# Sample-token convolution taps as GpSimd products with VectorE sums, and another order of projections in the first mixer

## The chip, the cores and the metric

The kernel runs on one core of a Trainium2 chip. The metric is the time of one execution on the device in microseconds (us), the median of 3 runs. The core's engines are called as the profile calls them: PE (TensorE; PEld is its weight load), DVE (VectorE), ACT (ScalarE), POOL (GpSimd), and SP (SyncE), which issues most transfers. Each takes its own instructions in one fixed order.

## What is computed

One inference step of a two-layer decoder trunk for 512 prompt tokens and 8 sequences of 4 sample tokens, 544 columns in all; the layout is channels on partitions, tokens along the free axis. Only the first layer's mixer is touched by the change. Cut to that:

```python
def causal_depthwise(ext, w, b):                 # 31 taps, one filter a channel
    y = lax.conv_general_dilated(ext, w[:, None, :].astype(ext.dtype), (1,), 'VALID',
                                 dimension_numbers=('NWC', 'WIO', 'NWC'),
                                 feature_group_count=ext.shape[-1])
    return y + b.astype(ext.dtype)

def mixer_ab(x, conv_st, shift_st, wkv_st, w_in, conv_w, conv_b, ln_g, ln_b, ...):
    p = x @ w_in
    pa, pb = p[..., :2 * D_A], p[..., 2 * D_A:]
    u = pa[..., :D_A] * jax.nn.sigmoid(pa[..., D_A:])
    ext = jnp.concatenate([conv_st.astype(u.dtype), u], axis=1)
    ya = jax.nn.silu(layer_norm(causal_depthwise(ext, conv_w, conv_b), ln_g, ln_b)).astype(f32)
    ...
    r, k, v, wl, al, gl = jnp.split(q, SPLIT_B, axis=-1)     # q: pb after the token shift
    ...
    y, new_wkv = wkv_recurrence(r, k, v, decay, kk, a, wkv_st)
    ...
    out = jnp.concatenate([ya, yb], axis=-1) @ w_out
```

The convolution has 512 channels (four tiles of 128), the recurrence 8 heads of 64 channels (four pairs of heads, one pair a tile).

## The kernel before, in words

The input projection has 22 tiles of 128 output channels: gates and values of the four convolutions (4 to 7 and 0 to 3), r, k and v of the four pairs (8 to 19), and two low-rank tiles (20, 21). A projection is a loop over 8 blocks of 128 input channels in two halves of the columns (256 and 288); each block takes three products (`xh` by `whi`, `xl` by `whi`, `xh` by `wlo`), since weights and inputs are split into a high and a low part. So one projection is 48 products on PE (line 192). The weights come as one stream in the order of `ab_order` (line 305). ACT makes each `whi`, and DVE the `wlo` that belongs to it.

The mixer is written as generators that are emitted in turns by `weave` (line 172): each step of a part has the priority of its turn plus the part's delay (`hi` -4, `md` -6, `lo` 8), and a scheduler then fixes the order of every engine's queue. The parts are these:

- `pair_in(p)`: projections of k, r and v of pair p; DVE and POOL make the operands `ar` and `kb` (line 439 on).
- `pair_front(p)`: PE's products of `ar` and `kb` (line 725) go through DVE to `xa` and `xk`. `xa` goes to DRAM as `dx` and comes back as `xb` by SP's queue, one 16x16 block a partition. POOL inverts the blocks there (`wkv_solve`, line 759) in 30 small steps (`stmp`, `mm`). The result goes back as `dm`, and to its place as `mn`.
- `pair_mid(p)`: PE's products with `mn`; the first of them (line 801) give DVE's `z`.
- `pair_out(p)`: the scan over eight chunks (line 882), group norm and gate, to `yb`.
- `conv_in(i)`: the projections of gate and value; DVE writes `uext` (prompt) and `usam` (30 rows of state and 4 new tokens of 8 sequences).
- `conv_taps(i)`: ACT's first tap and 30 DVE taps into `cacc`, for the prompt's 512 columns and for the samples' 32 columns each (line 167).
- `conv_end`: layer norm over the four convolutions, silu, and the half of the output projection that needs only them (8 tiles of 24 products). The second half needs every pair's `yb`.
- `sample_front`, `sample_out`: the recurrence of the sample tokens, with a solve of its own on POOL.

What holds the mixer's order are the fixed queues: PE meets products with `mn` between those of the projections, POOL has solves and operands in one queue, and DVE has taps, weight splits and evictions in one queue.

Of the kernel before, what the change touches and what calls it, by code (L numbers as in the profile page):

```python
# [15 lines left out]
P = 128  # L16
# [108 lines left out]
class Kernel:  # L125
# [46 lines left out]
    def weave(self, *gens):  # L172
        """emits the steps of (delay, part) in turns; the scheduler takes the step of least turn plus delay first"""
        gens = list(gens)
        while gens:
            for g in list(gens):
                try:
                    with self.tc.high_priority(offset=self.tc.cur_priority - int(200 * (self.turn + g[0]))):
                        next(g[1])
                except StopIteration:  # L180
                    gens.remove(g)
            self.turn += 1

    def order(self, ins):
        """the first product of a bank clears it, the others add to it, the last one ends it"""
        for a, b in [(ins[0], b) for b in ins[1:-1]] + [(a, ins[-1]) for a in ins[1:-1]]:
            self.tc.add_manual_dep(b.ins, a.ins.name, mybir.DependencyInfo(
                mybir.DependencyClass.NoSync, mybir.DependencyReason.DATA), reason="order")

    def mm(self, *a, **k):  # L190
        """a product; while `last` is not None, the tensor engine takes them as they are emitted"""
        ins = self.nc.tensor.matmul(*a, **k)  # L192
        if self.last is not None:
            self.chain(self.last + [ins])
            self.last = [ins]
        elif self.gates:
            # products of the layer norm go between those of the stream as soon as they can
            self.since += 1
            while self.gates and self.since > self.gates[0][0] + GWIDTH:
                self.gates.pop(0)  # L200
            for n, g in self.gates:
                if self.since > n:
                    self.chain([g, ins])
        return ins

    def dma(self, q, out, in_):
        """a transfer; while `lastq` is not None, the queue takes them as they are emitted"""
# [16 lines left out]
    def stream(self, key, ms, parts):  # L224
        """chunks of the m tiles `ms`, taken in turns"""
# [5 lines left out]
    def slot(self, which, i, name):  # L231
        """a tile for chunk i from the pool whose next tile frees first; None while that one is in use"""
# [35 lines left out]
    def gemm_steps(self, tiles, x, halves=(0, 1), look=2, turns=False, keep=False, parts=None, tags=("mm", "mm")):  # L268
        """products of the m tiles `tiles` [(key, m)], k in turns; x(k) -> (hi halves, lo halves)"""
# [27 lines left out]
    def setup(self):  # L297
# [6 lines left out]
        # tiles of w_in_ab: conv value 0-3, gate 4-7, r 8-11, k 12-15, v 16-19, wl|al 20, gl 21  # L304
        self.ab_order = [20, 21, 12, 8, 16, 4, 0, 13, 9, 17, 5, 1, 14, 10, 18, 6, 2, 15, 11, 19, 7, 3]
# [21 lines left out]
    # ================= layer 0: conv | wkv =================  # L327
    def mixer_ab(self):
# [52 lines left out]
        def shifted(m, ps, q):  # L381
            """token shift of tile m (of the RWKV part): q <- (1-mu) p + mu prev"""
# [22 lines left out]
        # until x comes back for the residual, its place holds what lives briefly  # L405
# [22 lines left out]
        def conv_taps(i):  # L428
# [5 lines left out]
            self.act(cs, usam[:, 0:32], AF.Identity, scale=w(0), bias=cb)  # L434
            for t in range(1, 31):
# [3 lines left out]
                self.stt(cs, usam[:, 8 * t:8 * t + 32], w(t), cs, ALU.mult, ALU.add)  # L439
            yield  # L440

        def pair_in(p):
# [17 lines left out]
            # inclusive sums of the log decay within chunks  # L460
# [22 lines left out]
            # keys and keys times rate of a chunk: those of even chunks the other way round  # L483
# [7 lines left out]
            # minus the normalized key, and the key times the in-context rate  # L491
# [19 lines left out]
            # sum over a head of r k r_k, times v  # L511
# [33 lines left out]
        def head_norm(y, parts, bv, gate, out, tag="wi"):  # L545
            """group norm of each head, plus bonus, times gate"""
# [42 lines left out]
        def conv_end():  # L589
            """layer norm over the 512 channels, swish, and what it adds to the residual"""  # L590
# [42 lines left out]
        weave((md, pair_front(0)), (0, conv_in(0)), (0, pair_in(1)))  # L633
        weave((hi, pair_mid(0)), (md, pair_front(1)), (0, conv_in(1)), (0, after(5, pair_in(2))), (lo, conv_taps(0)))
        weave((hi, pair_out(0)), (hi, pair_mid(1)), (md, pair_front(2)), (0, conv_in(2)), (0, after(4, pair_in(3))), (lo, conv_taps(1)))
        weave((hi, pair_out(1)), (hi, pair_mid(2)), (md, pair_front(3)), (0, conv_in(3)), (lo, conv_taps(2)))
        nc.scalar.dma_start(out=O["shift"], in_=shout)
        weave((hi, pair_out(2)), (hi, pair_mid(3)), (md, sample_front()), (lo, conv_taps(3)))
# [27 lines left out]
    def head_rsqrt(self, x, out, scale, v, tag, floor=True):  # L666
        """1 / sqrt(max(s, v)) or 1 / sqrt(s + v), s = scale times the sum over a head of x, on the head's channels"""
# [33 lines left out]
    # channels: (head, channel) on partitions. tokens: those of chunk c = 2 cp + c2 that go with alpha, b and w on  # L701
    # HS[c2], those that go with k and v on the other half
    def blocks(self):
        """chunk, its half, cp, where w and v keep it, head, rows of alpha, b and w, rows of k and v"""
# [4 lines left out]
    def wkv_front(self, d, dx):  # L709
        nc, gp = self.nc, self.gp  # L710
        ar, kb, v = d["ar"], d["kb"], d["v"]
        # per head and chunk: products with alpha and with r, then b and k themselves
# [20 lines left out]
        # tokens on partitions  # L733
# [25 lines left out]
    def wkv_solve(self, dx, dm, nu, mn):  # L759
        """inverses of the unit lower triangular 16-blocks and their transposes, one block a partition"""  # L760
# [30 lines left out]
    def wkv_mid(self, d):  # L791
        """from the inverses of the 16-blocks to (I - X)^-1, then its products with alpha and B"""
# [13 lines left out]
        # the inverses of the 32-blocks: of the first one as it is, of both transposed  # L806
# [13 lines left out]
        # the block between them  # L820
# [26 lines left out]
    def wkv_tail(self, d):  # L847
        nc, gp = self.nc, self.gp
        xk, R, wv, ar, pend = d["xk"], d["R"], d["wv"], d["ar"], d["pend"]
        # of chunk c = 2 cp + c2: [P, c2, cp, 64]  # L850
# [44 lines left out]
    # tokens of pair p on HS[p % 2]: 32 that go with alpha, b and w, then 32 that go with k and v  # L895
# [71 lines left out]
    def sample_end(self, g, ys):  # L967
# [7 lines left out]
        # r and alpha against the states  # L975
# [33 lines left out]
        # new states; what comes from tokens of other sequences is masked out  # L1009
# [18 lines left out]
    # ================= residual and layer norm =================  # L1028
# [10 lines left out]
    def norm_tile(self, m, ps, halves=(0, 1), scaled=False):  # L1039
        """z = ALPHA x + f (scaled: x comes with the factor), kept in xf less the mean of its first tile"""  # L1040
# [33 lines left out]
    def norm_end(self, name, layer, h, out=None):  # L1074
# [7 lines left out]
        with self.tc.high_priority(offset=UP):  # L1082
# [18 lines left out]
            # (y y v - 3) y is -2 times the next y  # L1101
# [48 lines left out]
    # ================= feed-forward =================  # L1150
# [11 lines left out]
    def ffn(self, L, out=None):  # L1162
        nc, tc, I, O = self.nc, self.tc, self.I, self.O
        with tc.tile_pool(name=f"ff{L}", bufs=1) as fp:
# [11 lines left out]
            def value(i, h, hp):  # L1176
                """silu of the causal convolution of half h"""
# [61 lines left out]
    # ================= layer 1: S5 =================  # L1239
    def s5_setup(self, new):  # L1240
        """the discretization; rows 0-63 and 64-127 both hold the 64 states; in the place of tiles written later"""
# [30 lines left out]
        # powers 0..8 of the transition  # L1272
# [13 lines left out]
        # f = (A - 1) / lambda  # L1286
# [14 lines left out]
        # q_j = A^(7-j) f, j = 0..7; p1 = (pr; -pr), p2 = (-pi; -pi), q1 = (qr; qr), q2 = (-qi; qi)  # L1301
# [14 lines left out]
        # eight steps turn by this much, in turns; against it on the rows of imaginary parts  # L1316
# [4 lines left out]
        # sample: A^4 h0  # L1321
# [13 lines left out]
    def s5_systems(self):  # L1335
        """the matrices of all tiles, in the place of the activations, which nothing reads meanwhile"""
# [19 lines left out]
        for m in range(8):  # L1356
# [17 lines left out]
            # impulse responses, 4 groups side by side  # L1374
# [23 lines left out]
    def mixer_c(self, ctx, yp):  # L1398
# [13 lines left out]
        # inputs: states on rows  # L1412
# [9 lines left out]
        def rotations(m):  # L1422
            """by 1..64 times eight steps"""
# [12 lines left out]
        def load_fm(m, q):  # L1436
            """matrices of the 8 groups of tile m: what comes in"""
# [3 lines left out]
        def load_gx(m, q):  # L1441
            """from the states to what goes out"""
# [3 lines left out]
        def load_tm(m, q):  # L1446
            """from what comes in to what goes out"""
# [5 lines left out]
        def value(m, h, ps):  # L1453
            """half h of u: steps of eight on rows"""
# [18 lines left out]
        def states(m):  # L1473
            """what comes in, rotated"""
# [15 lines left out]
        def swapped(e):  # L1490
            """real and imaginary parts exchanged"""
# [159 lines left out]
    def _exp(self, out, x):  # L1651
        """e^x to float32's accuracy: 2^k e^r"""
# [19 lines left out]
    def _sincos(self, sp, x, sn, cs, turns):  # L1672
        """sine and cosine of x, and x in turns less whole ones"""
        V = self.nc.vector
        k, r, z, s, c = (sp() for _ in range(5))
        # quarter turns
# [19 lines left out]
        # quarter q = k mod 4: angle = r + q pi/2, in turns k/4 + r/(2 pi)  # L1696
        V.tensor_scalar(turns, k, 0.25, None, op0=ALU.mult)
        self._frac(turns)  # in -1/2..1/2: -1/2 (or 1/2), -1/4, 0, 1/4
        a, b = self._new(), self._new()
        # cos(q pi/2) = 1 - 4 |t|  and sin(q pi/2) from t  # L1700
        self.stt(a, turns, -1.0, turns, ALU.mult, ALU.max)
        V.tensor_scalar(a, a, -4.0, 1.0, op0=ALU.mult, op1=ALU.add)
        # sin: 4 t where |t| = 1/4, else 0: 4 t (1 - |cos|)
# [155 lines left out]
```

## Time and profile before

| | |
|---|---|
| median of 3 runs | 1547.79 us (1545.06 to 1548.09) |
| the profiled execution's own time (its span) | 1542.7 us |
| its mean granted TensorE clock | 0.953 of 2.4 GHz |
| busy: PE, PEld, DVE, ACT, POOL | 94 %, 89 %, 66 %, 40 %, 23 % of the span |
| first mixer (up to the second half of the output projection) | 0 to 380.93 us |

The span is counted from the first to the last instruction of one profiled execution, while the median belongs to runs without a profile; the two differ by 5.1 us. Busy shares are averages over stages: the mixer that the change touches is a quarter of the span, and its shares are read from stretches of 50 us. An instruction's wait is named by what released it.

### The profile page before, as it was taken

How to read it: one execution, taken by the hardware profiler on the slowest of the kernel's cores; microseconds unless marked ns; L12 is line 12 of the kernel's file. 1: busy time of each engine (PE TensorE's matmuls, PEld its weight loads, DVE VectorE, ACT ScalarE, POOL GpSimd, SP SyncE). 2: the span in 40 equal slices, each digit the busy share in tenths (PEclk: the TensorE clock that was granted, in tenths of full speed). 3: DMA queues.
4: the chain of work that ended last, by engine and by line, in shares of the span. 5: the costliest groups of instructions: out<-in, count | busy, mean ns of one | idle time of the engine just before them, and what ended most of it. 6: DMA issues, size and time to landing. Idle time of an engine off the chain costs nothing.

```text
span 1542.7 us, 31307 instructions
## 1 busy us (share of the span) xinstructions
PE 1445.0 (94%) x12064; PEld 1374.1 (89%) x12064; DVE 1013.4 (66%) x2513; ACT 616.9 (40%) x1407; POOL 353.9 (23%) x492
## 2 busy tenths in 40 slices
PE   7999999789799999999999789999899999999996
PEld 6988887577789999999899778899899999999996
DVE  6688796766879955557884856754675555554335
ACT  5444352251264444443232435553454444442222
POOL 1252552611540200002561622102420000000102
PEclk9999999689899999999999789999999999999997
DMA  5222113111213232225563367832222222232321
GB/s 192 73 65 67 39 54 100 22 38 58 99 37 118 89 127 89 84 85 164 165 182 116 111 178 210 219 107 96 67 69 89 90 89 85 88 92 86 84 68 58
DMA packets 128340, 152.43 MB, mean 99 GB/s; under 512 B 46512, under 2 KB 71856, under 8 KB 127936
## 3 DMA queue, kind: packets, MB, share of 16 engines
q1 hardware_dynamic: 105232, 120.11, 25.7%
q10 hardware_dynamic: 20800, 22.46, 4.6%
q0 software_dynamic: 2160, 7.87, 1.6%
q8 instruction: 95, 1.56, 0.4%
q14 instruction: 53, 0.43, 0.1%
HBM read 128.17 MB, written 22.22 MB: 97 GB/s over the span
## 4 chain that ended last, share of the span: by engine, by line
PE 71%; DVE 11%; DMA 6%; POOL 4%; issue 3%; ACT 3%; SPq 1%; ACTq 0%; DVEq 0%; POOLq 0%
PE ps_mm L192 61%; PE ps_wk L192 3%; POOL stmp L170 2%; DVE xres L170 2%; POOL mm L170 2%; DVE wlo L170 2%; DVE xres L167 1%; DMA tm<-dk 1%; DVE s5a L170 1%; PE ps_wf L725 1%; ACT xres L164 1%; DVE ln_t L167 1%; PE ps_wk L1089 1%; DMA dg<-s5a 1%; DMA ye<-dy 1%
## 5 line engine op out<-in xcount | busy, mean ns | idle before, releaser
L192 PE MATMUL ps_mm<-xh,whi 128*128 128x256 f32 (+1 forms) x2016 | 492.1, 298 | 21.9 <-ACT whi L262 6.5
L192 PE MATMUL ps_mm<-xl,whi 128*128 128x256 f32 (+1 forms) x2016 | 493.2, 296 | 5.2 <-DVE xl L167 3.6
L192 PE MATMUL ps_mm<-xh,wlo 128*128 128x256 f32 (+1 forms) x2016 | 490.0, 295 | 0.0
L170 DVE TENSOR_TENSOR wlo<-wraw,whi 128x512 fp32r<-128x512 f32 x350 | 258.4, 740 | 272.3 <-ACT whi L262 270.1
L262 ACT CAST whi<-wraw 128x512 fp32r<-128x512 f32 x380 | 230.9, 611 | 514.7 <-PE ps_mm L192 448.9
L192 PEld LDWEIGHTS ps_mm<-xh,whi 128*128 128x128 f32 x2016 | 353.6, 195 | 29.4 <-ACT whi L262 6.8
L192 PEld LDWEIGHTS ps_mm<-xl,whi 128*128 128x128 f32 x2016 | 356.9, 195 | 14.3 <-issue 5.9
L192 PEld LDWEIGHTS ps_mm<-xh,wlo 128*128 128x128 f32 x2016 | 354.3, 194 | 4.6 <-issue 3.9
L192 PE MATMUL ps_mm<-fl,whi 128*128 128x256 f32 (+1 forms) x704 | 154.3, 290 | 0.0
L192 PE MATMUL ps_mm<-fh,whi 128*128 128x256 f32 (+1 forms) x704 | 153.7, 289 | 0.0
L192 PE MATMUL ps_mm<-fh,wlo 128*128 128x256 f32 (+1 forms) x704 | 153.6, 289 | 0.0
L192 PEld LDWEIGHTS ps_mm<-fh,wlo 128*128 128x128 f32 x704 | 115.7, 188 | 0.7 <-issue 0.6
L192 PEld LDWEIGHTS ps_mm<-fl,whi 128*128 128x128 f32 x704 | 115.8, 188 | 0.4 <-issue 0.4
L192 PEld LDWEIGHTS ps_mm<-fh,whi 128*128 128x128 f32 x704 | 115.5, 188 | 0.7 <-issue 0.6
L167 DVE SCALAR_TENSOR_TENSOR c<-ps_mm,cols,c 128x254 f32<-128x254 f32 (+3 forms) x264 | 98.1, 393 | 0.3
L167 DVE SCALAR_TENSOR_TENSOR cacc<-uext,cols,cacc 128x512 f32<-128x512 f32 x120 | 94.8, 790 | 2.5 <-ACT cacc L164 1.5
L170 POOL TENSOR_TENSOR ln_s<-xres 128x256 f32<-128x256 f32 (+1 forms) x8 | 10.3, 1301 | 313.8 <-DVE xres L170 313.8
L170 DVE TENSOR_TENSOR s5a<-s5a 128x64 f32<-128x64 f32 (+3 forms) x135 | 74.5, 574 | 9.0 <-DMA dg<-s5a 4.4
L170 DVE TENSOR_TENSOR c<-ps_mm,c 128x256 f32<-128x256 f32 (+1 forms) x88 | 35.3, 435 | 60.3 <-PE ps_mm L192 54.6
L170 POOL TENSOR_TENSOR s5a<-s5a 128x1024 f32<-128x1024 f32 (+2 forms) x19 | 48.1, 2532 | 49.9 <-DVE s5a L170 44.2
L170 POOL TENSOR_TENSOR wlo<-wraw,whi 128x512 fp32r<-128x512 f32 x30 | 41.5, 1390 | 77.7 <-ACT whi L262 74.2
L192 PE MATMUL ps_mm<-yh,whi 128*128 128x256 f32 (+1 forms) x240 | 57.4, 293 | 0.3 <-ACT sg L164 0.3
(368 smaller groups left out, 2064.2 us busy)
## 6 DMA issues: line engine op xcount, KB each, us to landing
wraw<-in_w_up SPq DMA_DIRECT2D x176, 256.0 KB
wraw<-in_w_down SPq DMA_DIRECT2D x80, 256.0 KB
wraw<-in_w_in_ab SPq DMA_DIRECT2D x44, 256.0 KB
wraw<-in_w_out_c SPq DMA_DIRECT2D x21, 256.0 KB
wraw<-in_w_out_ab SPq DMA_DIRECT2D x16, 256.0 KB
dg<-s5a ACTq DMA_DIRECT2D x8, 512.0 KB
df<-s5a ACTq DMA_DIRECT2D x8, 512.0 KB
gx<-dg POOLq DMA_DIRECT2D x8, 512.0 KB, 5.1
```

Of the source, the lines that this page charges most:

```text
L164: return self.nc.scalar.activation(out, in_, f, **k)
L167: return self.nc.vector.scalar_tensor_tensor(out, a, s, b, op0, op1)
L170: return (eng or self.nc.vector).tensor_tensor(out, a, b, op=op)
L192: ins = self.nc.tensor.matmul(*a, **k)
L262: self.nc.scalar.copy(hi, src)
L725: nc.tensor.matmul(pa[:, i], lhsT=flat(kb[HS[hd], c // 2, c % 2]), rhs=ar[HS[hd], :, c], start=True, stop=True)
L1089: gate = nc.tensor.matmul(pq[:, 4 * i + j:4 * i + j + 1], lhsT=t[:, b - P:b], rhs=self.con("ones")[:, 0:1], start=t is ts[0], stop=t is ts ...
```

## The change

Two things are changed, both in the first mixer. The samples' taps of a convolution, one ACT operation and 30 DVE operations of 128x32, become two GpSimd products (`spr`: a window of the 31 rows for two of the four tokens, by the weights, 128x496), two VectorE sums over the 31 taps (128x496 to 128x16), and one ACT bias add. And the order of the projections changes: those of the pairs 1 to 3 stand two places earlier, those of the convolutions 0 to 2 behind them; each `conv_in` and each `conv_taps` goes into the weave one stage later, and the taps of the last convolution get a weave of their own.

```diff
-        self.ab_order = [20, 21, 12, 8, 16, 4, 0, 13, 9, 17, 5, 1, 14, 10, 18, 6, 2, 15, 11, 19, 7, 3]
+        self.ab_order = [20, 21, 12, 8, 16, 13, 9, 17, 4, 0, 14, 10, 18, 5, 1, 15, 11, 19, 6, 2, 7, 3]
...
             self.act(ca, uext[:, 0:NP], AF.Identity, scale=w(0), bias=cb)
-            self.act(cs, usam[:, 0:32], AF.Identity, scale=w(0), bias=cb)
+
+            at = usam[:, 0:8]
+            o = COL["caw"] + i * 31
+            ws = self.cols[:, o:o + 31].unsqueeze(1).unsqueeze(1).broadcast_to([P, 2, NS, 31])
+            for j in range(0, NJ, 2):
+                pr = gp.tile([P, 2, NS, 31], F32, name="spr", tag="spr", bufs=1)
+                win = bass.AP(at.tensor, at.offset + NS * j, [at.ap[0], (NS, 2), (1, NS), (NS, 31)])
+                self.tt(pr, win, ws, ALU.mult, nc.gpsimd)
+                nc.vector.tensor_reduce(cs[:, NS * j:NS * j + 2 * NS].rearrange("p (j s) -> p j s", s=NS), pr,
+                                        mybir.AxisListType.X, ALU.add)
+            self.act(cs, cs, AF.Identity, bias=cb)
             for t in range(1, 31):
                 if t % 8 == 0:
                     yield
                 self.stt(ca, uext[:, t:t + NP], w(t), ca, ALU.mult, ALU.add)
-                self.stt(cs, usam[:, 8 * t:8 * t + 32], w(t), cs, ALU.mult, ALU.add)
             yield
...
         weave((0, pair_in(0)))
-        weave((md, pair_front(0)), (0, conv_in(0)), (0, pair_in(1)))
-        weave((hi, pair_mid(0)), (md, pair_front(1)), (0, conv_in(1)), (0, after(5, pair_in(2))), (lo, conv_taps(0)))
-        weave((hi, pair_out(0)), (hi, pair_mid(1)), (md, pair_front(2)), (0, conv_in(2)), (0, after(4, pair_in(3))), (lo, conv_taps(1)))
-        weave((hi, pair_out(1)), (hi, pair_mid(2)), (md, pair_front(3)), (0, conv_in(3)), (lo, conv_taps(2)))
+        weave((md, pair_front(0)), (0, pair_in(1)))
+        weave((hi, pair_mid(0)), (md, pair_front(1)), (0, conv_in(0)), (0, after(2, pair_in(2))))
+        weave((hi, pair_out(0)), (hi, pair_mid(1)), (md, pair_front(2)), (0, conv_in(1)), (0, after(2, pair_in(3))), (lo, conv_taps(0)))
+        weave((hi, pair_out(1)), (hi, pair_mid(2)), (md, pair_front(3)), (0, conv_in(2)), (lo, conv_taps(1)))
         nc.scalar.dma_start(out=O["shift"], in_=shout)
-        weave((hi, pair_out(2)), (hi, pair_mid(3)), (md, sample_front()), (lo, conv_taps(3)))
+        weave((hi, pair_out(2)), (hi, pair_mid(3)), (md, sample_front()), (0, conv_in(3)), (lo, conv_taps(2)))
+        weave((lo, conv_taps(3)))
         weave((hi, pair_out(3)), (hi, sample_out()), (0, conv_end()))
```

How the queues move, at three places. In the rows a name's number tells its buffer; the arrow points from what is read to what is written.

DVE at the start of the kernel, before. `usam` are the samples' windows of the first two convolutions, `wlo` is a weight's low part, `wa` the low-rank input that PE needs first:

```order
L167 SCALAR_TENSOR_TENSOR cacc_168<-usam_1235,cols_69,cacc_168 128x32
L167 SCALAR_TENSOR_TENSOR cacc_168<-usam_648,cols_69,cacc_168 128x32
L170 TENSOR_TENSOR wlo_260<-wraw_187,whi_259 128x512
L167 SCALAR_TENSOR_TENSOR cacc_168<-usam_1235,cols_69,cacc_168 128x32
L167 SCALAR_TENSOR_TENSOR cacc_168<-usam_648,cols_69,cacc_168 128x32
L167 SCALAR_TENSOR_TENSOR wa_179<-ps_mm_181,cols_69,wa_179 128x256
L167 SCALAR_TENSOR_TENSOR wa_179<-ps_mm_182,cols_69,wa_179 128x255
```

The same place now:

```order
L170 TENSOR_TENSOR xl_73<-xin_153,xh_71 128x256
L170 TENSOR_TENSOR xl_74<-xin_153,xh_72 128x288
L170 TENSOR_TENSOR wlo_260<-wraw_187,whi_259 128x512
L167 SCALAR_TENSOR_TENSOR wa_179<-ps_mm_181,cols_69,wa_179 128x256
L167 SCALAR_TENSOR_TENSOR wa_179<-ps_mm_182,cols_69,wa_179 128x255
```

The sample taps that the queue held among the splits of x (`xl`) and ahead of `wa` are gone.

DVE about the last convolution's product (`uext_2949`, `usam_2950`), before. `xa_2929` and `xk_2930` are pair 3's evictions, two of four here, and the two others follow:

```order
L170 TENSOR_TENSOR xa_2929<-ps_wf_2933,cons0_88 128x256
L170 TENSOR_TENSOR xk_2930<-ps_wf_2933,cons0_88 128x4x64
L170 TENSOR_TENSOR wlo_4169<-wraw_2965,whi_4168 128x512
L170 TENSOR_TENSOR uext_2949<-ps_mm_3092,xres_75 128x256
L170 TENSOR_TENSOR usam_2950<-ps_mm_3092,xres_75 128x32
L170 TENSOR_TENSOR wlo_4213<-wraw_3097,whi_4212 128x512
L167 SCALAR_TENSOR_TENSOR cacc_168<-usam_2950,cols_69,cacc_168 128x32
L167 SCALAR_TENSOR_TENSOR y_1596<-y_1596,cols_69,ps_wi_2794 128x512
L167 SCALAR_TENSOR_TENSOR cacc_168<-usam_2950,cols_69,cacc_168 128x32
L170 TENSOR_TENSOR xa_2929<-ps_wf_2940,cons0_88 128x256
```

The same place now, with pair 3's evictions as `xa_2708`, the last convolution as `uext_3300` and `usam_3301`, and the one before it as `uext_2728`:

```order
L170 TENSOR_TENSOR xa_2708<-ps_wf_2860,cons0_88 128x256
L170 TENSOR_TENSOR xk_2709<-ps_wf_2860,cons0_88 128x4x64
L167 SCALAR_TENSOR_TENSOR cacc_168<-uext_2728,cols_69,cacc_168 128x512
L167 SCALAR_TENSOR_TENSOR rq_t_2646<-rq_t_2646,rq_x_2644 128x8
L170 TENSOR_TENSOR wlo_4073<-wraw_3316,whi_4072 128x512
L167 SCALAR_TENSOR_TENSOR cacc_168<-uext_2728,cols_69,cacc_168 128x512
L170 TENSOR_TENSOR uext_3300<-ps_mm_3441,xres_75 128x256
L167 SCALAR_TENSOR_TENSOR rq_y_2645<-rq_t_2646,rq_y_2645 128x8
L170 TENSOR_TENSOR usam_3301<-ps_mm_3441,xres_75 128x32
L170 TENSOR_TENSOR wlo_4117<-wraw_3446,whi_4116 128x512
L167 SCALAR_TENSOR_TENSOR cacc_168<-uext_2728,cols_69,cacc_168 128x512
L167 SCALAR_TENSOR_TENSOR st_2681<-ps_wb_2682,pend_647,xp_2307 128x64
```

The first row of this piece is the last of pair 3's four `xa`: they moved ahead of the last convolution's product, and the taps of the convolution before it, 17 of 30, moved behind.

POOL ahead of pair 3's solve, before. `stmp` and `mm` are the solve, `k`, `kb`, `skb` the operands of pair 3, the `xres<-cacc` rows the first sums of `conv_end`, `st` a state of the scan:

```order
L170 TENSOR_TENSOR kb_2739<-k_2554,xres_75 128x4x64 x2
L170 TENSOR_TENSOR skb_171<-k_2554,rps_2503 128x32
L170 TENSOR_TENSOR xres_75<-cacc_168 128x256
L170 TENSOR_TENSOR xres_75<-xres_75,cacc_168 128x256
L170 TENSOR_TENSOR xres_75<-cacc_168 128x288
L170 TENSOR_TENSOR yb_169<-yb_169,v_2819 128x544
L170 TENSOR_TENSOR xres_75<-xres_75,cacc_168 128x288
L878 COPY st_3499<-xp_3325 128x64
L170 TENSOR_TENSOR stmp_3359<-xb_3357,mm_3358 64x15
```

The same place now, with `ar` another operand of pair 3:

```order
L170 TENSOR_TENSOR k_2230<-k_2230,xres_75 128x544
L888 COPY st_2681<-xp_2307 128x64
L170 TENSOR_TENSOR spr_3372<-usam_2729,cols_69 128x496
L170 TENSOR_TENSOR kb_2476<-k_2230,xres_75 128x4x64 x2
L170 TENSOR_TENSOR skb_171<-k_2230,rps_2170 128x32
L170 TENSOR_TENSOR ar_2475<-r_2231,xres_75 128x512
L170 TENSOR_TENSOR spr_3784<-usam_3301,cols_69 128x496
L170 TENSOR_TENSOR spr_3787<-usam_3301,cols_69 128x496
L170 TENSOR_TENSOR stmp_3114<-xb_3112,mm_3113 64x15
```

Both products of the last convolution's samples stand directly ahead of pair 3's solve; the sums of `conv_end` stood there, and now come later.

## Rows read from the trace of the kernel before

**Rows 1.** The page, part 1: busy time (share of the span), instructions of each engine.

```profile
PE 1445.0 (94%) x12064; PEld 1374.1 (89%) x12064; DVE 1013.4 (66%) x2513; ACT 616.9 (40%) x1407; POOL 353.9 (23%) x492
```

**Rows 2.** Busy time by stretches: us, PE, PEld, DVE, ACT, POOL (instructions), clock, DMA share, GB/s.

```profile
0.00:50.00 50.00, 41.06 (x268) 37.57 (x269) 31.32 (x110) 29.12 (x65) 7.20 (x25) 0.97 0.46 159
...
250.00:300.00 50.00, 40.53 (x492) 30.18 (x488) 41.80 (x96) 12.71 (x29) 24.17 (x43) 0.81 0.24 61
...
450.00:700.00 250.00, 250.00 (x1990) 250.00 (x1989) 169.98 (x562) 110.33 (x280) 11.84 (x20) 1.00 0.30 100
```

**Rows 3.** Chain of waits, 0 to 400 us: start, us, what (count).

```profile
19.02 1.46 DVE cacc L167 x9
```

**Rows 4.** PE's waits, 0 to 400 us: us in total, times, longest.

```profile
PE ps_wo L801 <- DMA mn<-dm: 12.4, 5, 3.8
...
PE ps_mm L192 <- DVE wa L167: 2.3, 1, 2.3
```

**Rows 5.** PE's timeline: start, us, operation [idle before and its releaser].

```profile
319.63 0.58 PE L192 MATMUL ps_mm<-xh,whi 128*128 128x256 f32 x1 [1.97 <-ACT xh L262]
...
380.93 0.58 PE L192 MATMUL ps_mm<-xh,whi 128*128 128x256 f32 x1 [1.40 <-DVE yb L170]
```

**Rows 6.** Chain of waits, 255 to 300 us.

```profile
264.11 0.66 DVE cacc L167
...
265.44 1.03 DVE cacc L167
...
268.38 0.34 DVE xa L170
268.75 2.13 DMA dx<-xa
...
273.45 2.04 DMA xb<-dx
276.37 0.69 POOL stmp L170
```

**Rows 7.** POOL's timeline: the first operation of solves 0, 1, 3; the end of 0.

```profile
91.74 0.22 POOL L170 TENSOR_TENSOR stmp<-xb,mm 64x15 f32<-64x15 f32 x1 [3.66 <-DMA xb<-dx]
...
111.58 0.62 POOL L782 COPY mm<-mm 64x256 f32<-64x256 f32 x1
...
153.69 0.21 POOL L170 TENSOR_TENSOR stmp<-xb,mm 64x15 f32<-64x15 f32 x1
...
275.79 0.21 POOL L170 TENSOR_TENSOR stmp<-xb,mm 64x15 f32<-64x15 f32 x1 [2.69 <-DMA xb<-dx]
```

**Rows 8.** DVE's timeline: `usam` of the last convolution, taps, `xa`, the last tap, `z`.

```profile
257.20 0.18 DVE L170 TENSOR_TENSOR usam<-ps_mm,xres 128x32 f32<-128x32 f32 x1
...
257.99 0.24 DVE L167 SCALAR_TENSOR_TENSOR cacc<-usam,cols,cacc 128x32 f32<-128x32 f32 x1
258.15 0.75 DVE L167 SCALAR_TENSOR_TENSOR y<-y,cols,ps_wi 128x512 f32<-128x512 f32 x1
...
268.30 0.42 DVE L170 TENSOR_TENSOR xa<-ps_wf,cons 128x256 f32<-128x256 f32 x1
...
296.11 0.75 DVE L167 SCALAR_TENSOR_TENSOR cacc<-uext,cols,cacc 128x512 f32<-128x512 f32 x1
...
306.29 0.68 DVE L170 TENSOR_TENSOR z<-ps_wo,cons 128x512 f32<-128x512 f32 x1
```

**Rows 9.** All taps, by tile: ns shortest/middle/longest, first and last start, form.

```profile
L167 DVE SCALAR_TENSOR_TENSOR cacc<-usam,cols,cacc x120: 226/243/1348, 16.3 to 262.2; 128x32 f32<-128x32 f32 x120
L167 DVE SCALAR_TENSOR_TENSOR cacc<-uext,cols,cacc x120: 718/744/1817, 66.6 to 296.1; 128x512 f32<-128x512 f32 x120
```

**Rows 10.** DVE's groups by form, 0 to 450 us: busy, mean ns | idle before.

```profile
L467 DVE TENSOR_TENSOR_SCAN xres<-cons,xres 128x256 f32<-128x256 f32 x8 | 5.5, 684 | 1.0 <-ACT xres L164 1.0
...
L612 DVE RECIPROCAL xres<-xres 128x288 f32<-128x288 f32 x1 | 1.9, 1943 | 0.0
```

**Rows 11.** POOL's groups by form, whole span.

```profile
L170 POOL TENSOR_TENSOR s5a<-s5a 128x1152 f32<-128x1152 f32 x8 | 20.3, 2539 | 33.0 <-DVE s5a L170 33.0
L170 POOL TENSOR_TENSOR ang<-tab,cons 128x512 f32<-128x512 f32 x8 | 11.1, 1398 | 16.9 <-DVE e L170 16.9
L170 POOL TENSOR_TENSOR yb<-yb,v 128x544 f32<-128x544 f32 x4 | 6.0, 1500 | 22.1 <-ACT yb L517 22.1
```

**Rows 12.** POOL's solve steps by tile, 0 to 450 us.

```profile
L170 POOL TENSOR_TENSOR stmp<-xb,mm x75: 203/285/859, 91.7 to 316.0; 64x15 f32<-64x15 f32 x8, 64x28 f32<-64x28 f32 x8, 64x39 f32<-64x39 f32 x8, 64x48 f32<-64x48 f32 x8
```

## The prediction, made before the changed kernel ran

> **What bounds the kernel now.** The page comes first [rows 1]: TensorE (PE) is busy 94 % of a span of 1542.7 us, VectorE (DVE) 66 %, GpSimd (POOL) 23 %. A table by stretches comes next [rows 2]: from 450 to 700 us PE is busy all the time at the full granted clock (1.00 of 2.4 GHz), so what the change does to the later stages is left out, and only the first mixer, up to the second half of the output projection at 380.93 us [rows 5], counts. There PE's holes are at the start (41.06 of 50 us busy) and from 250 to 300 us (40.53 of 50, granted clock 0.81); in the latter DVE is busiest too (41.80), and POOL has 24.17 us. So the reader should look for two things: what PE waits for at the start, and what pair 3 waits for near 250 to 300 us.
>
> At the start nine sample taps stand in the chain of waits, 1.46 us from 19.02 [rows 3], and PE then waits 2.3 us for `wa` on DVE [rows 4]. The list of PE's waits is led by `mn`, 12.4 us in 5 waits [rows 4]: the inverses that POOL computes for each pair and sends through DRAM. The chain of 255 to 300 us [rows 6] shows what pair 3's `mn` hangs on: DVE's taps (`cacc`) in turns with the evictions `xa`, then from 268.75 us the DMAs of `dx` and `xb`, then POOL's solve from 275.79 us [rows 7], and its `mn`.
>
> **The change part by part: the engines.** Removed on DVE: 120 sample taps of 128x32, 0.243 us in the middle [rows 9], 29 us. Queued ones start only 0.16 us after each other (257.99, then the next operation at 258.15 [rows 8]), so they hold DVE for 20 us at least; I take 25. On ScalarE 4 first taps go and 4 bias adds of the same size come: nothing.
>
> Added on DVE: 8 sums over taps, 128x496 in and 128x16 out. No row shows one. From below, a 128x256 scan of 0.684 us reads half as much; from above, a reciprocal of 288 elements takes 1.943 us [rows 10]. I take 0.75, the value of a 512-wide tap (0.744 [rows 9]), since a sum too passes some 500 elements once: 6 us, ends 4 and 15. Added on POOL: 8 products of 128x496 with one factor broadcast. The nearest row, 128x512 with a broadcast factor (`ang`), takes 1.40 us; a 128x1152 product 2.54 [rows 11]. I take 1.4, 11 us in all, ends 9 and 20, the upper one because the window is read at a stride. So DVE is rid of some 19 us net (5 to 25), most of it between 90 and 300 us, and POOL takes on 11.
>
> **The start.** In the new DVE order no tap stands ahead of `wa`; 17 sample taps of two convolutions went, most of which filled waits for x, and two first taps on ScalarE. The bounds are 0 and the whole wait, 2.3 us; I take -1.5, about the nine taps in the chain.
>
> **The pairs.** The projections of pairs 1 to 3 stand two places earlier, those of the convolutions later. One projection is 48 products of 0.126 us (250 us over 1990 [rows 2]), 6 us, so a pair may begin 12 us earlier. What does not move with them is POOL: solve 0 begins when `xb` is there (91.74 us) and ends with its copy at 111.58 + 0.62 [rows 7]; two tap products (2.8 us) now stand in it. Pair 1's operands on POOL are queued behind it, so solve 1 (153.69 us before [rows 7]) comes some 9 us earlier, not 12. PE's products with pair 1's `mn` stand more than two projections earlier in its queue, so it waits there longer: 12.4/5 = 2.5 us on average before, now 5 to 12. From there to the same products of pair 2 PE has work without a gap, the same as before or a little more, and pair 2 is reached at its old time within some 4 us. Nothing is won by then but the start.
>
> Pair 3 is different. Before, the last of its four `xa` came at 268.30, among the taps and 11 us behind the last convolution's `usam` (257.20) [rows 8]. In the new order all four stand ahead of that `usam`. POOL has that convolution's two tap products in front of solve 3, so the solve can begin at some 257 + 1 + 2.8 = 261 us instead of 275.79, if the last `xa` is out by 254 (from `dx` to the solve's start are 7 us [rows 6, 7]). DVE sets how much of these 14 us is kept: from pair 2's `z` to pair 3's its queue holds the same work in both orders, within 2 us by my count of its rows, while in 250 to 300 us it had 8 us idle. Pair 3's `z` was made at 306.29 us [rows 8]; I take 8 us earlier, between 0 and 12.
>
> **The convolution's tail** goes the other way. Behind the last `usam` the old order had 30 prompt and 30 sample taps of one convolution, and ended them at 296.11 + 0.75 [rows 8], 39.7 us later. The new one has 17 prompt taps of convolution 2 and the 30 of convolution 3 by its rows: 17 more of 0.744 are 12.6 us, less 30 sample taps (5 to 7), less two `xa` and `xk` (1.5), plus two sums (1.5) and the work of pair 3 that moves into this stretch (4 to 8). So the last tap comes 10 to 14 us later, at 305 to 309 us with the start's gain, and at 300 to 319 by the ends of the costs. The first product of the output projection, at 319.63 before [rows 5], comes as much later. Has it room? Its first half, 192 products, needs 192 x 0.126 = 24 us alone, and there were 61 us up to 380.93; the other 37 are pair 3's scan, the samples and waits, most of which do not need it. A little under half of them PE works for others, so I give the tail 14 us of room: last tap up to 311, first output product up to 334. With the pairs at -8 and the tail inside its room by 2 to 6 us, the mixer's end moves by between -8 and -1; I take -4.3, start included.
>
> **Sum.** 1542.7 - 4.3 = 1538.4. The median of the runs, 1547.79, stands 5.1 above the profiled span, so I forecast **1543.5 us**. A measurement of this kernel tells about 0.2 %, 3.1 us, from no change.
>
> **A rule against the sum.** The prompt taps have a middle of 0.744 us and a longest of 1.817 [rows 9], POOL's `stmp` 0.285 and 0.859 [rows 12]: something makes single ones more than twice as long. The Trainium skill, "SBUF — State Buffer", section "Who interferes with whom", says that a VectorE instruction with two SBUF inputs and a GpSimd instruction that reads SBUF contend for one shared pair of ports, and that the loser blocks for the whole instruction. The trace fits that rule, and by it each new product could hold up a tap for its full length, 8 x 1.4 = 11 of the 19 us that DVE wins.
>
> **Rivals.** (a) *The tail ends it* (slower): should the last tap come past 311 us, each further us costs one. At 319, which needs the upper ends of the sums and of the taps in this stretch, the end is 8 us later, less the start's 1.5: 1554. For it: DVE is busiest just there [rows 2]. Against: 8 us of it are idle there.
> (b) *Given back* (no change): PE's longer wait for pair 1's `mn` (10 to 12 us), and a lower granted clock after it, as the 0.81 beside PE's idle 9.5 us in 250 to 300 us [rows 2], eat the start and what pair 3 wins: 1547.5. For it: POOL's solve 1 moves 3 us less than the projections. Against: this holds for pair 1 alone.
> (c) *DVE stands at the sums* (slower): DVE takes its queue in order, and each sum waits for a product that POOL has behind other work (`yb`, 1.5 us [rows 11], or a solve), or that a tap holds up. If the 8 sums stop DVE for 2 us each, 16 of the 19 us are lost, the tail comes at some 317 us, and the end is 5 us later: 1553. It decides from about 1.5 us a sum.
>
> That the change does not do what it says is no rival: the new orders show the sample taps gone and the products in place.
>
> **Chances.** The forecast, with a larger gain up to -16 (1532: all of pair 3's 14 us kept), 0.47; (b) 0.21; (a) 0.20; (c) 0.12. So faster by over 0.2 % 0.47, within it 0.21, slower 0.32. The range goes from 1531 (the larger gain) to 1557 ((a) with 11 us for 8); the likeliest case's own is 1535 to 1545.
>
> **What would show it.** Right: PE's wait for `wa` under 1 us; solve 3 begins before 266 us, and pair 3's `z` comes before 300; the last tap between 304 and 311; the output projection begins by 334, and the mixer ends between 373 and 380; a product on POOL of 1.2 to 1.6 us, a sum of 0.6 to 0.9. Wrong: PE waits over 12 us for pair 1's `mn`; the last tap after 315 us; sums that wait over 1.5 us each for their products; PE out of work before a first output product after 334 us.

## The result, and the profile after

The changed kernel took 1570.96 us, median of 4 runs (1560.47 to 1578.82), against 1546.42 us for the kernel before in the same comparison: a ratio of 1.0134 (the two medians alone give 1.0159), with a 95 % interval of 1.0094 to 1.0174. The forecast was 1543.5 us, at most 1557: wrong in sign and outside its range. The profiled execution, the fastest of the four, has a span of 1558.7 us, 16.0 more than before, and nearly all of that is there when the layer norm behind the mixer ends. PE's timeline shows the wait for `wa` at the start and the last wait before the uninterrupted stretch of products, in the kernel before:

```profile
21.86 0.61 PE L192 MATMUL ps_mm<-xh,whi 128*128 128x288 f32 x1 [2.26 <-DVE wa L167]
...
444.14 0.40 PE L192 MATMUL ps_mm<-xl,whi 128*128 128x288 f32 x1 [1.03 <-DVE xl L167]
```

and in the changed kernel, with two places between them:

```profile
21.19 0.41 PE L192 MATMUL ps_mm<-xh,whi 128*128 128x288 f32 x1 [2.06 <-DVE wa L167]
...
156.36 0.45 PE L811 MATMUL ps_wo<-mn,xa 64*64 64x64 f32 x2 [6.60 <-DMA mn<-dm]
...
344.82 0.58 PE L192 MATMUL ps_mm<-xh,whi 128*128 128x256 f32 x1
...
459.33 0.40 PE L192 MATMUL ps_mm<-xl,whi 128*128 128x288 f32 x1 [1.03 <-DVE xl L167]
```

So 15.2 us are lost by then (the "mark" below: 444.14 to 459.33). The wait for `wa` stayed (2.06 us against 2.26), pair 1's `mn` keeps PE 6.60 us (with 1.06 soon after), and the output projection begins at 344.82, not 319.63 [rows 5]. Where the time goes shows in the table by stretches of the changed kernel (columns as in [rows 2]):

```profile
150.00:200.00 50.00, 41.83 (x429) 34.95 (x430) 25.80 (x46) 12.84 (x29) 17.16 (x25) 0.76 0.14 29
200.00:250.00 50.00, 44.56 (x405) 41.41 (x403) 36.53 (x67) 18.32 (x40) 24.60 (x44) 0.97 0.32 87
250.00:300.00 50.00, 41.16 (x474) 31.42 (x474) 46.12 (x91) 12.73 (x29) 24.34 (x39) 0.77 0.23 61
300.00:350.00 50.00, 42.00 (x538) 32.50 (x538) 42.11 (x95) 19.59 (x48) 22.19 (x42) 0.70 0.09 17
```

From 150 to 200 us PE is short of work, its granted clock is 0.76, and DVE is half idle (25.80); DVE then has 46.12 and 42.11 of 50 us from 250 on. The same table, of the projections' products alone (tile `ps_mm`; columns: stretch, its us, then PE, PEld, DVE, ACT, clock, DMA share, GB/s), says what is missing. Before:

```profile
150.00:200.00 50.00, 22.69 (x151) 19.98 (x152) 2.04 (x7) 2.48 (x9) 0.97 0.19 50
200.00:250.00 50.00, 25.47 (x161) 22.27 (x160) 3.39 (x10) 2.98 (x10) 0.93 0.25 65
```

After:

```profile
150.00:200.00 50.00, 15.68 (x74) 13.16 (x74) 0.95 (x3) 0.47 (x1) 0.76 0.14 29
200.00:250.00 50.00, 35.89 (x254) 33.85 (x254) 4.15 (x12) 3.97 (x14) 0.97 0.32 87
```

74 products in place of 151: the 77 missing ones, some one and a half projections of 48, were not done while PE ran small products of pairs 1 and 2, and were made up in a lump. DVE's timeline of the changed kernel has the consequence:

```profile
267.72 0.19 DVE L170 TENSOR_TENSOR usam<-ps_mm,xres 128x32 f32<-128x32 f32 x1
...
268.42 1.99 DVE L167 SCALAR_TENSOR_TENSOR cacc<-uext,cols,cacc 128x512 f32<-128x512 f32 x1
...
271.26 0.66 DVE L442 TENSOR_REDUCE cacc<-spr 128x16 f32<-128x496 f32 x1
...
311.87 0.68 DVE L170 TENSOR_TENSOR z<-ps_wo,cons 128x512 f32<-128x512 f32 x1
...
321.67 0.74 DVE L167 SCALAR_TENSOR_TENSOR cacc<-uext,cols,cacc 128x512 f32<-128x512 f32 x1
```

The last `usam` comes 10.5 us later than before, pair 3's `z` 5.6 us later, and the last tap 25.6 us later [rows 8]. On POOL, solve 1 begins 16.6 us earlier and solve 3 only 1.8 us earlier [rows 7], behind two tap products:

```profile
137.14 0.21 POOL L170 TENSOR_TENSOR stmp<-xb,mm 64x15 f32<-64x15 f32 x1 [3.01 <-DMA xb<-dx]
...
268.04 1.82 POOL L170 TENSOR_TENSOR spr<-usam,cols 128x496 f32<-128x496 f32 x1 [18.23 <-issue]
272.00 2.01 POOL L170 TENSOR_TENSOR spr<-usam,cols 128x496 f32<-128x496 f32 x1 [2.14 <-DVE rq_t L167]
273.96 0.66 POOL L170 TENSOR_TENSOR stmp<-xb,mm 64x15 f32<-64x15 f32 x1
```

The new operations by tile (ns shortest/middle/longest): a product takes 1.945 us in the middle, a sum 0.656 us.

```profile
L170 POOL TENSOR_TENSOR spr<-usam,cols x8: 1556/1945/2011, 91.5 to 272.0; 128x496 f32<-128x496 f32 x8
L442 DVE TENSOR_REDUCE cacc<-spr x8: 654/656/670, 93.5 to 275.9; 128x16 f32<-128x496 f32 x8
```

### The profile page after: what moved, and what is told of

Its sections match the earlier page's. It is cut to its first block, busy times and chain, and to the rows that moved or that the text cites. A ratio compares the mean times of both kernels' runs of the same rounds, so it can differ in the third digit from the quotient of the medians.

```text
span 1558.7 us, 31227 instructions
## 1 busy us (share of the span) xinstructions
PE 1452.8 (93%) x12064; PEld 1380.8 (89%) x12064; DVE 998.4 (64%) x2401; ACT 616.5 (40%) x1407; POOL 366.6 (24%) x500
## 4 chain that ended last, share of the span: by engine, by line
PE 62%; DVE 11%; DMA 4%; issue 3%; POOL 2%; ACT 2%; ACTq 0%; DVEq 0%; SPq 0%; POOLq 0%
PE ps_mm L192 54%; PE ps_wk L192 3%; DVE xres L170 2%; DVE wlo L170 2%; DVE xres L167 1%; DVE cacc L167 1%; DVE s5a L170 1%; DMA dg<-s5a 1%; DVE ln_t L167 1%; PE ps_wk L1099 1%; ACT xres L164 1%; POOL stmp L170 1%; POOL mm L170 1%; DMA wraw<-in_w_in_c 0%; DMA tm<-dk 0%
## 5 line engine op out<-in xcount | busy, mean ns | idle before, releaser
L167 DVE SCALAR_TENSOR_TENSOR cacc<-uext,cols,cacc 128x512 f32<-128x512 f32 x120 | 99.6, 840 | 1.0
```

The source lines that it names most:

```text
L167: return self.nc.vector.scalar_tensor_tensor(out, a, s, b, op0, op1)
```

## The experiments

Theory T at first: convolutions come later, so their taps end the mixer late. Rivals: G (the GpSimd products), P (PE's wait for pair 1's `mn`). Ratios are to the kernel before, with 95 % intervals. Timed runs of one kernel spread by 7 to 24 us, so verdicts go by ratios, and profiles, one execution each, serve for places. From the mark to the end, which no edit touches, the profiled executions took 1098.6 to 1111.3 us, so the mark tells more of the mixer than the span does.

**The taps alone** (`e1_taps`): the changed `conv_taps`, with `ab_order` and the weaves as before.

> The new sample taps (GpSimd products, VectorE sums) in the old order of projections and stages. Theory T (the convolutions, moved later, end the mixer late): the taps themselves take some 20 us off VectorE and cost little, so this kernel is 0 to 6 us faster than before, about 1543. Rival G (the GpSimd products of 1.95 us and the sums that wait for them make the loss): slower than before by 6 to 20 us, and solves that start later than 275.79 us.

1.0018 (0.9988 to 1.0048): no difference that can be told. The interval alone, up to 7 us slower, leaves room for G's 6 us; but the mark was at 441.13 us, 3.0 early, and solve 3 began at 267.20, not after 275.79 as G has it. So nothing speaks for G in the old order.

**The order alone** (`e2_order`): the new `ab_order` and weaves, `conv_taps` as before.

> The new order of projections and stages with the old sample taps on VectorE. Theory T: 12 to 30 us slower than before, and the last prompt tap comes after 315 us. Rival G: within 5 us of before.

0.9989 (0.9966 to 1.0012), mark 437.39, 6.8 us early. T falls: the later convolutions cost nothing by themselves, and the last tap comes at 304.65, not after 315 us. Neither part makes the loss; both together do. The two kernels with the new order emit the same products for PE, but the scheduler, with other work on DVE and POOL to plan for, ordered PE's queue differently: between the first products with pair 0's and with pair 1's `mn` stand 4.1 projections before, 3.0 here, and 1.9 in the changed kernel; from there to pair 2's `mn` stand 4.2, 6.1 and 6.8.

**A shorter tail** (`e3_tail`), most columns of taps 11 to 30 of two convolutions left out:

```diff
-                self.stt(ca, uext[:, t:t + NP], w(t), ca, ALU.mult, ALU.add)
+                n = 64 if i >= 2 and t > 10 else NP
+                self.stt(ca[:, 0:n], uext[:, t:t + n], w(t), ca[:, 0:n], ALU.mult, ALU.add)
```

> The changed kernel, leaving out most of the columns (448 of 512) of prompt taps 11 to 30 of convolutions 2 and 3: 40 taps some 0.45 us shorter, 18 us less work for VectorE behind the last projections. Theory T: the mixer's end follows the last tap, 10 to 16 us faster than the changed kernel. Rival P (TensorE's lost time at pair 1's mn, 150 to 200 us, is what counts, and the tail is hidden): less than 4 us faster.

1.0092 (1.0058 to 1.0125), some 6 us below the changed kernel's ratio, with overlapping intervals, so the runs do not settle it. In the profile the mark is at 450.14, 9.2 us earlier, and the output projection's `xl` 20 us earlier: the tail seems to carry a part of the loss, not all of it. The scheduler also ordered PE's queue otherwise from 269 us on, so this run does not show the tail alone.

**A shorter solve for pair 1** (`e4_mn1`):

```diff
-            yield from self.wkv_solve(dx, dm, 8, self.mn)
+            yield from self.wkv_solve(dx, dm, 8, self.mn, 3 if p == 1 else 15)
...
-        for j in range(15):
+        for j in range(steps):
```

> The changed kernel, leaving out the last 12 of 15 steps of pair 1's solve on GpSimd; TensorE's order is the same instruction by instruction. The solve is 9 to 11 us shorter, so TensorE's wait of 6.6 us for pair 1's mn goes, and the half clock after it perhaps too. Rival P: 6 to 12 us faster than the changed kernel, and the last convolution's usam back from 267.7 to about 258 us. Theory T in its narrow form (only the number of taps behind the last projection counts): less than 4 us faster.

1.0118 (1.0081 to 1.0156), mark 461.30: nothing gained that can be told. The wait is gone (PE's products with `mn` start at 151.10 without one), yet from 150 to 200 us the clock is 0.80 and the projections' products are 96, not 151. All instructions from 150 and from 250 us, then the projections' products from 150 us:

```profile
150.00:200.00 50.00, 47.95 (x507) 39.33 (x504) 29.88 (x52) 18.15 (x39) 20.63 (x31) 0.80 0.14 36
250.00:300.00 50.00, 41.89 (x428) 32.79 (x429) 38.60 (x75) 10.58 (x24) 24.34 (x39) 0.64 0.14 37
```

```profile
150.00:200.00 50.00, 17.95 (x96) 14.89 (x97) 0.93 (x3) 0.47 (x1) 0.80 0.14 36
```

Taking the wait away did move PE: pair 2's `z` comes at 249.12, 5.5 us earlier than in the changed kernel. But that lead was lost again: from 250 to 300 us the clock is 0.64 against 0.77, the last `usam` comes at 270.20, where P had 258, and pair 3's `z` at 314.35, 2.5 us later. The intervals would still hide a gain of some 10 us. So the wait's length does not account for the loss by itself, and this run does not rule it out as a part. It made theory S: what PE's queue holds there is the cause, and the wait a symptom.

**PE's queue exchanged** (`e5_pe_of_e2`, `e6_pe_of_after`). The changed kernel gets the order-only kernel's (e2's) order of the first mixer's 2436 products in PE's queue (e5), and the other way round (e6). Holding a kernel to its own order leaves all queues as they were; holding it to the other's moves the other engines' queues too, since the scheduler plans them about PE's.

```diff
+PE_ORDER = [...]   # by number of emission, read from the other kernel's built queue
...
         self.mixer_ab()
+        self.chain([LOG[i] for i in PE_ORDER[:len(LOG)]])
```

> The changed kernel with TensorE's queue in the first mixer held, product by product, to the order that the order-only kernel had. All else of the change stays: GpSimd products, sums, new order of projections. Theory S (the cheaper taps let the scheduler draw pairs 1 and 2 together among fewer projections, so that TensorE runs small products at half clock from 150 to 200 us and the projections fall behind): back to 1538 to 1548 us, granted clock over 0.9 from 150 to 200 us, last usam near 256 us. Rival G (the GpSimd products and the sums cost it, but only under the new order): stays above 1558 us.

> The converse: the order-only kernel (old sample taps on VectorE, no GpSimd products) with TensorE's queue in the first mixer held to the changed kernel's order. Theory S: 1558 to 1575 us, clock under 0.85 from 150 to 200 us, last usam after 265 us. Rival G: stays near the order-only kernel, 1540 to 1550 us.

The changed kernel with the order-only kernel's PE queue: 1.0049 (1.0023 to 1.0075), mark 446.02. The order-only kernel with the changed kernel's PE queue: 1.0077 (1.0050 to 1.0104), mark 458.32, and no GpSimd product in it. So the exchange moves the time by 0.85 % one way (1.0134 to 1.0049; as an estimate from the intervals, plus or minus 0.5) and 0.88 % the other (0.9989 to 1.0077; plus or minus 0.35), 13 us. The marks, of the order-only kernel, e5 and e6:

```profile
437.39 0.40 PE L192 MATMUL ps_mm<-xl,whi 128*128 128x288 f32 x1 [1.03 <-DVE xl L167]
```

```profile
446.02 0.40 PE L245 MATMUL ps_mm<-xl,whi 128*128 128x288 f32 x1 [1.03 <-DVE xl L220]
```

```profile
458.32 0.40 PE L248 MATMUL ps_mm<-xl,whi 128*128 128x288 f32 x1 [1.03 <-DVE xl L223]
```

The projections' products follow the queue. In the order-only kernel and, with its queue, in the changed kernel (e5):

```profile
150.00:200.00 50.00, 23.00 (x149) 20.66 (x150) 2.63 (x8) 2.18 (x8) 0.93 0.22 52
```

```profile
150.00:200.00 50.00, 21.66 (x147) 18.82 (x146) 1.95 (x6) 1.98 (x6) 1.00 0.20 50
```

and with the changed kernel's queue in the order-only kernel (e6):

```profile
150.00:200.00 50.00, 13.07 (x57) 10.78 (x57) 0.95 (x3) 0.00 (x0) 0.76 0.14 29
```

147 products at full clock against 57 at 0.76; the last `usam` of e6 comes at 267.73, where the changed kernel's does, and its mark 1.0 us before that kernel's. S holds for the larger part of the loss. What was exchanged is PE's order with what the scheduler then makes of the other queues: read from the traces up to 460 us, sample taps left out, e6's DVE, ACT and POOL have 92, 98 and 96 % of their operations in the changed kernel's order, and 72, 81 and 67 % in the order-only kernel's.

But e5 stayed above what S expected: some 0.6 % over the order-only kernel. Its median, 1558.26 us beside 1549.74 of the kernel before, is above S's 1548 and just above G's 1558; e6, which loses without a GpSimd product, and e8 below speak against G.

**The tap products on DVE**: with a free scheduler (`e7_dve`), with the order-only PE queue (`e8_dve_pe`), and in the old order (`e9_dve_old`).

```diff
-                self.tt(pr, win, ws, ALU.mult, nc.gpsimd)
+                self.tt(pr, win, ws, ALU.mult)
```

> The changed kernel with the tap products on VectorE (0.69 us each by its 512-wide rows) instead of GpSimd (1.95 us); the scheduler is free. It now puts 3.3 projections between TensorE's first products for pair 0's and pair 1's mn (the changed kernel 1.9, the order-only kernel 2.95). Theory S plus a smaller cost of the GpSimd products: 1536 to 1548 us, clock over 0.9 from 150 to 200 us. Rival (any new order of this kind is 10 us slower, whatever TensorE's queue): above 1556 us.

> As the run before, with TensorE's queue held to the order-only kernel's. If the 0.6 % by which the run with TensorE's order put back stayed above the order-only kernel is GpSimd's products (in the solves of pairs 0 and 3), it goes here: 1536 to 1547 us, no slower than the order-only kernel. If it stays (above 1553 us), it is not GpSimd's.

> The old order of projections and stages with the sample taps as products and sums, both on VectorE. VectorE has some 11 us of products and sums in place of 20 to 29 us of taps, GpSimd nothing new, TensorE's queue hardly moves: 2 to 8 us faster than before (1540 to 1546). No change if nothing in this mixer but the pairs' chain counts.

e7: 1.0065 (1.0043 to 1.0087), a miss. Its stretch from 150 to 200 us is sound (clock 1.00), but PE has another hole, a wait of 14.59 us of the samples' products that ends with ACT's `xk` of pair 3; that this hole makes its loss was not shown:

```profile
285.79 0.58 PE L925 MATMUL ps_wf<-sar,skb 64*64 64x64 f32 x5 [14.59 <-ACT xk L766]
```

e8: 1.0047 (1.0022 to 1.0071), like e5's 1.0049: what was left over stays when GpSimd has no tap product. e9: 0.9973 (0.9952 to 0.9993), mark 441.01: faster than the kernel before, by 0.07 to 0.48 %, and so than the changed one.

**A shorter solve for pair 0** (`e10_mn0`), e8 with 10 of 15 steps for pair 0. In e8 and e5 PE waits 3.08 and 4.72 us for pair 0's `mn`, in the order-only kernel 1.29, and the clock from 100 to 150 us is 0.90, 0.86 and 1.00.

> The run with tap products on VectorE and TensorE's queue held to the order-only kernel's, leaving out the last 5 of 15 steps of pair 0's solve, so that pair 0's mn comes some 5 us earlier; TensorE's queue is the same. Theory W (TensorE, no longer late at the start, now waits 3 to 5 us for pair 0's mn, and runs at half clock after it, and this is the 0.5 % that was left): no wait there, granted clock 1.00 from 100 to 150 us (0.90 in the run before), solve 1 from 143.7 back to 139 us or earlier, and 4 to 9 us faster, near the order-only kernel's 1545. If the time does not move (within 3 us), what was left lies elsewhere, in the other queues' orders behind 250 us.

1.0014 (0.9990 to 1.0037), against e8's 1.0047: 5 us, within what W expected, but the two intervals overlap and stand in different comparisons, so this gain is not shown. No wait, clock 0.97 (W had 1.00), pair 1's `z` at 161.71 and not 166.02. In the profiles only 2.1 us of that reach the mark (450.91 to 448.77), and e10's PE still waits 5.93 us for pair 3's `mn`. Against the order-only kernel, whose PE queue it has, e10 makes pair 2's `z` 3.0 us earlier (236.44 and 239.44) and reaches the mark 11.4 us later. In e5 pair 2's `z` is 2.9 us late (242.30), pair 3's 9.2 (300.05 and 290.89), the mark 8.6. So by these profiles (one execution each, e10's the slowest of its twelve) most of the remainder arises behind pair 2's `z`, not where W has it. Why stays open; that an order of PE that was planned for other work on DVE costs time as such was not tested.

## Why the prediction was wrong, point by point

- **The start**, -1.5 forecast: the product that waits for `wa` starts at 21.19, not 21.86, and those behind it come 0.13 us apart, not 0.24, so that the thirteenth starts at 22.88, not 24.91: -2.0, inside its bounds. But `wa` still kept PE 2.06 us, where the prediction looked for less than 1: the taps ahead of it had mostly filled waits. So the size is near by luck.
- **The pairs: the step that failed.** "From there to the same products of pair 2 PE has work without a gap ... and pair 2 is reached at its old time within some 4 us." It had work, but the wrong kind: 74 products of projections against 151, and small ones at a mean granted clock of 0.76, which of the two levels, 1.2 and 2.4 GHz, is nearly half of the stretch at the lower. Nor was it "the same as before or a little more": from pair 1's `mn` to pair 2's PE had 6.8 projections, not 4.2. Pair 2's `z` came at 254.63 us against 242.69. I took the two places by which the stream of projections moved for all that moved in PE's queue; how the small products are spread among the projections was there to be counted (4.1 before, 1.9 now between the first uses of `mn`), and I counted it only as an earlier wait. That wait is all that I priced (5 to 12 us; 7.7 measured), and taking it away (e4) gave no gain that can be told.
- **Pair 3**, 8 us earlier forecast: `z` 5.6 us later. Solve 3 began at 273.96, not 261: the last projection was late by 10.5 us, and the second product waited for the first sum, which ended at 271.92 (one buffer).
- **The tail**, 10 to 14 us later forecast: 25.6, of which 10.5 are the late projection and 15 the taps behind it (54.7 us from `usam` to the last tap, 39.7 before): the number of taps was near, its start was not. The room of 14 us is not shown. With the new order a later last tap mostly goes with a later mark (against the kernel before, +8.5 and -6.8 us in e2, +15.2 and +1.9 in e5, +22.9 and +14.2 in e6, +25.6 and +15.2 here), but e3 (+5.7 and +6.0) and e7 (+8.2 and +7.5) lose at the mark with a tail inside that room.
- **The sizes**: a product 1.945 us (1.4 taken, 20 us for all as upper end; 15 measured), most of the excess a wait for VectorE (last section), a sum 0.656 (0.75 taken). Neither decides (e1, e8).
- **From span to median**, 5.1 us in the sum: 12.3, since the profiled execution was the fastest of the four.
- **The rivals**: (a) named the last tap past 311 us as the mechanism of a loss, and it came to pass, for another reason than it gave. (b)'s lower clock after the wait was seen, as part of the same thing. (c) fell: DVE waited 1.4 us in all for tap products.
- **The rule on the shared ports.** The tap at 268.42 took 1.99 us while the product of 268.04 ran until 269.86, and ended 0.55 us after it. The Trainium skill, "SBUF — State Buffer", section "Who interferes with whom", has such a pair of instructions block each other. This row agrees, and so do five more: at six of the eight products a VectorE operation took 1.80 to 2.21 us and ended 0.55 us after the product. By the usual lengths of these operations (0.68 to 0.74) that is some 7.6 us of DVE, near the 11 by that rule; in e1, with eight products too, no loss can be told from it.

## What to carry to other kernels

Where a scheduler fixes the queues, a change in a cheap part can reorder the critical engine's queue: compare that queue first, and count what fills each wait (here, projections between two uses of `mn`), not only where a step moved. A wait on the critical engine can be the mark of a thin queue; take it away by itself before believing that its length is the loss, and follow the lead that this gives to the end of the stage. To part a change from its side effect on the order, hold one engine's queue to the other kernel's order: here that moved the time by 0.85 %, while each part of the change alone showed no difference. Then look at what the scheduler made of the other queues, which move with it.

## What the runs showed of the hardware

A product that reads a window at a stride of 32 bytes took 1.06 us on DVE, where a contiguous 512-wide one (`wlo`) takes 0.69. From e9, by tile:

```profile
L170 DVE TENSOR_TENSOR spr<-usam,cols x8: 1032/1062/1134, 63.6 to 261.7; 128x496 f32<-128x496 f32 x8
```

On POOL it took 1.95 us in the middle, against 1.40 for the nearest row [rows 11], but that is mostly not the stride. In e1 one product ran while DVE stood still, waiting for it, and took 1.46 us:

```profile
110.38 1.46 POOL L170 TENSOR_TENSOR spr<-usam,cols 128x496 f32<-128x496 f32 x1
111.87 0.67 DVE L442 TENSOR_REDUCE cacc<-spr 128x16 f32<-128x496 f32 x1 [1.94 <-POOL spr L170]
```

In the changed kernel the product of 268.04 began while DVE ran an operation with two inputs in SBUF:

```profile
267.82 0.68 DVE L170 TENSOR_TENSOR wlo<-wraw,whi 128x512 fp32r<-128x512 f32 x1
```

That one ended at 268.50, and the product 1.35 us behind it. Four more products of the changed kernel (91.47, 185.47, 189.27 and 272.00) began beside such an operation and ended 1.33 to 1.37 us behind its end. The Trainium skill, "GPSIMD Engine Reference", section "Performance pitfalls for Q7 kernels", puts such reads at half as much again on GpSimd, an estimate of 2.1 us from 1.40; the 1.46 us of the product that ran alone do not bear that out.

PE's granted clock went with what its queue held: from 150 to 200 us it was 0.76 with 57 to 76 of the wide products among the small ones (the changed kernel, e3, e6), 0.80 with 96 (e4, without PE's wait and with PE busy 47.95 of 50 us), and 0.93 to 1.00 with 147 to 180 in the eight other kernels. How much of the loss is this clock and how much the order of the work was not parted.
